# The S5 transfer tables laid out contiguously by a ScalarE copy, and the low halves of all head weights subtracted on VectorE, in a one-core hybrid decoder step

## The chip, the core and the metric

The program runs on one core of one Trainium2 chip. The metric is the time of one execution on the device in microseconds, as the median of several executions. Each engine (TensorE as PE, with its weight loads shown apart as PEld; VectorE as DVE; ScalarE as ACT; GpSimd as POOL; SyncE as SP, which only issues DMAs here) works through its own instructions in the order in which the program lists them, and waits where an input or a buffer isn't ready.

## What is computed

One decoder layer for 512 prompt tokens (with 16 meta tokens ahead of them) and 8 running sequences of 4 tokens, at width 1024. Two branches run beside each other on the projected input and are merged: HGRN2, a gated linear recurrence with 8 heads, and S5, a diagonal state-space model in 64 groups of 16 channels and 64 states. After them comes PEER, a mixer that picks 16 of 16384 single-neuron experts per head and token. Cut to the part around the change:

```python
proj = rmsnorm(x, norm1_w) @ w_in
q, f, i, g, u, ga, gb = split(proj)
o, s_new = hgrn2_scan(silu(q), 1 - fg, i, log(fg), s_hg)      # 8 heads of 128
y, x_re, x_im = s5_scan(u, ...)   # x_t = a_bar * x_(t-1) + b_bar u_t ;  y = Re(c x) + d u
x = x + (sigmoid(ga) * br_a + sigmoid(gb) * br_b) @ w_out
x = x + peer(rmsnorm(x, norm2_w), ...)
```

S5 is computed in blocks of 8 time steps. For each group a 128x128 table T (8 steps x 16 channels squared) gives what the inputs of a block add to the outputs of the same block, a table W gives what the state at the block's start adds, and AT gives the block's addition to the state.

## The kernel before

**Weight stream.** All dense products use 128x1024 weight tiles in fp32, split into two fp32r halves: `wh` is the tile cast on ACT (L434) and `wl` is tile minus `wh` (L435), on the engine that the job names. `Stream.run` takes the jobs in order. Job i multiplies its 8 blocks (`products`, L469: wh by hi, wh by lo, wl by hi, with two column halves each). Before its first product it issues the fetch, the cast and the subtraction for job i+1. `wh`, `wl` and the raw tile have two buffers each. After each quarter of a job the stream ticks two lists of background generators, `bg` and `fill`, and each tick issues one piece of such a generator to all engines.

**Jobs.** First come 8 jobs of S5's input u, then the 8 heads with 4 jobs each (F, Q, V, G: gate, query, value, output gate; F1 is the F job of head 1), then 8 each of GA, BA, GB, GLU, BB and WO. `N_EV = 1` puts the subtraction of head 0 on VectorE; heads 1 to 7 have it on GpSimd.

**Beside the heads.** While a head's jobs run, `bg` works on the head before (`head`): seven levels of `aps` matmuls on PE (L605, L612), each followed on DVE by the update of `h_qF` (L624) and `f_kB` (L625) that the next level's matmul reads. `fill` runs `s5_setup`, which makes the tables for eight sets of 8 groups: E, AT and W on DVE (L369, L371), a 128x128 piece `T7`, and then eight DMAs (`load(Ts[o % 2]...)`) that place shifted pieces of T7 in T with the group innermost, so that neighbouring elements of one group's table are 4 elements (16 bytes) apart. T goes to DRAM as it is (`Td`). `fill` also runs `rotations`, many small GpSimd operations (L286 to L293).

**S5 units.** From GA3 on, 16 units of four groups each run in `bg` (`s5_units`). A unit loads T, W, AT and its inputs, and its output is

```python
for g in range(4):
    mm(pyv[:, g], T[:, g], U[:, g, m0 : m0 + ny], start=True, stop=False)
    mm(pyv[:, g], W[:, g], xs[:, g, m0 : m0 + ny], start=False, stop=True)
```

with T or W as the stationary operand (L790, L791). In fp32 each of these matmuls runs as two passes. T is read through a view with a step of 4 elements; W is contiguous.

Of the kernel before, what the change touches and what calls it, by code (L numbers as in the profile page):

```python
# [8 lines left out]
F32 = mybir.dt.float32  # L9
# [10 lines left out]
P = 128  # L20
# [6 lines left out]
G = 64  # L27
# [63 lines left out]
def body(tc, a):  # L91
    nc = tc.nc
    mm = nc.tensor.matmul
    V, PO, AC = nc.vector, nc.gpsimd, nc.scalar
# [8 lines left out]
    def load(dst, src):  # L103
        nc.sync.dma_start(dst, src)
# [90 lines left out]
    Td = dram.tile([8, P, 2, 4 * P], F32, name="Td")  # L195
# [8 lines left out]
    def s5_setup(pm, qr):  # L204
# [42 lines left out]
            V.tensor_scalar(c, c, -2.0, 1.0, ALU.mult, ALU.add)  # L247
        t1 = sm("t1")
        q = pool(s5, "s5c", 1, True)
        Ts = [q.tile([P, 2, 8, 16, 4], F32, name=f"T{i}") for i in range(2)]  # L250
        u1, u2 = (T.rearrange("p a s c g -> p (a s c g)")[:, : 4 * G].rearrange("p (n g) -> p n g", g=G) for T in Ts)

        def cmul(outr, outi, ar, ai, br, bi, n):
            a, b = u1[:, :n], u2[:, :n]
# [77 lines left out]
        for e in (1, 2, 4):  # L332
            o, i = slice(8 - 2 * e, 8 - e), slice(8 - e, 8)
# [4 lines left out]
        V.tensor_copy(s5c["a4s"][64:128], pim[64:128, 4])  # L338
        V.tensor_scalar(s5c["a4s"][0:64], pim[0:64, 4], -1.0, None, ALU.mult)

        for T in Ts:
            PO.memset(T, 0.0)

        def params(o):
            r = {}
# [3 lines left out]
            return r  # L349

        def store(o):
            load(Td[o], Ts[o % 2].rearrange("p a s c g -> p a (s c g)"))

        nx = params(0)
        yield
# [1 line left out]
        for o in range(8):  # L357
            gs = slice(8 * o, 8 * o + 8)
            p, nx = nx, (params(o + 1) if o < 7 else None)
            V.tensor_scalar(p["b2"], p["b2"], sgn, None, ALU.mult)  # L360
            V.tensor_scalar(p["ct1"], p["ct1"], nsgn, None, ALU.mult)
            V.tensor_scalar(p["ct2"], p["ct2"], -1.0, None, ALU.mult)
            AT = q.tile([P, 8, P], F32, name="AT", tag="AT", bufs=2)
            E = q.tile([P, 8, 8, 16], F32, name="E", tag="E")
            W = q.tile([P, 8, 8, 16], F32, name="W", tag="W", bufs=2)
            for x, u, w, cr, ci in ((E, "b1", "b2", gr[:, :, gs], gi[:, :, gs]), (W, "ct1", "ct2", pr[:, 1:, gs], pim[:, 1:, gs])):
                xv, tmp = x.rearrange("p g s c -> p s g c"), AT.rearrange("p g (s c) -> p s g c", s=8)
                for dst, pp, cc in ((xv, p[u], cr), (tmp, p[w], ci)):
                    V.tensor_tensor(dst, pp.unsqueeze(1).to_broadcast([P, 8, 8, 16]), cc.unsqueeze(3).to_broadcast([P, 8, 8, 16]), ALU.mult)  # L369
                    yield  # L370
                V.tensor_tensor(xv, xv, tmp, ALU.add)  # L371
                yield
            Ec = E.rearrange("p g s c -> p g (s c)")
            T7 = q.tile([P, 2, 16, 4], F32, name="T7", tag="T7")
            T7v = T7.rearrange("p a c g -> p a g c")
            if o > 0:
                store(o - 1)
            V.tensor_tensor(T7v, p["dsk"].rearrange("p (a g) c -> p a g c", a=2), ident[:, 112:128].unsqueeze(1).unsqueeze(1).to_broadcast([P, 2, 4, 16]), ALU.mult)
            yield
            pt = pm.tile([P, 8, 16], F32, name="pt", tag="m")  # L380
            for i in range(8):
                mm(pt[:, i], Ec[:, i], p["ct1"][:, i], start=True, stop=True)
            V.tensor_tensor(T7v, T7v, pt.rearrange("p (a g) c -> p a g c", a=2), ALU.add)
            for hf in range(2):
                pt = pm.tile([P, 4, P], F32, name="pt", tag="m")
                for i in range(4):
                    nc.tensor.transpose(pt[:, i], Ec[:, 4 * hf + i], ident)
                AC.copy(AT[:, 4 * hf : 4 * hf + 4], pt)
                yield
            load(Wd[o], W.rearrange("p g s c -> p g (s c)"))  # L390
            for s in range(8):
                load(Ts[o % 2][0 : 16 * (s + 1), :, s], T7[16 * (7 - s) : 128])
                if s % 2:
                    yield
            load(ATd[o], AT)
# [304 lines left out]
    def s5_units(ph, pm, sp, Ud, Yd, units):  # L700
# [25 lines left out]
        for n_, u in enumerate(units):  # L726
            o, hf = u // 2, u % 2
            g4 = slice(4 * hf, 4 * hf + 4)
            gs = slice(4 * u, 4 * u + 4)
            r, nxt = nxt, None  # L730
            U, rc, rs = r["U"], r["rc"], r["rs"]
            T, W, xs = st("T", P), st("W", P), st("xs", nxs)
            load(T.rearrange("p g n -> p (g n)"), Td[o][:, hf])
            T = T.rearrange("p g n -> p (g n)").rearrange("p (n g) -> p g n", g=4)
            load(W, Wd[o][:, g4])
            if ph.sample:
                xw0 = st("xw0", 8)
                load(xs[:, :, nch:nxs], a["x0"][:, gs])
                load(xw0, a["x0w"][:, gs])
            if n_ + 1 < len(units):  # L740
                nxt = loads(units[n_ + 1])
            px = pm.tile([P, 512], F32, name="px", tag="m")
            pxv = px[:, : 4 * nu].rearrange("p (g n) -> p g n", n=nu)
            for g in range(4):
                mm(pxv[:, g], r["AT"][:, g], U[:, g], start=True, stop=True)
            X = st("X", nu)
            AC.copy(X, pxv)
            d0 = st("d0", nch)
            PO.tensor_copy(d0, s5c["rho"][:, gs].unsqueeze(2).to_broadcast([P, 4, nch]))
            PO.memset(d0[:, :, 0:1], 0.0)  # L750
            if ph.first:
                PO.memset(xs[:, :, 0:1], 0.0)
            else:
                PO.tensor_copy(xs[:, :, 0], sstate[:, gs])
            yield

            def swap(src):
                t = pm.tile([P, 512], F32, name="pxs", tag="m")
                tv = t[:, : 4 * nch].rearrange("p (g n) -> p g n", n=nch)
                mm(tv, T_["perm"], src, start=True, stop=True)  # L760
                return tv

            xw = swap(X[:, :, :nch])
            Z, t2, z, zc = st("Z", nch), st("t2", nch), st("z", nch), st("zc", nch)
            V.tensor_tensor(Z, X[:, :, :nch], rc[:, :, 1 : nch + 1], ALU.mult)
            V.tensor_tensor(t2, xw, rs[:, :, 1 : nch + 1], ALU.mult)
            V.tensor_tensor(Z, Z, t2, ALU.subtract)
            if not ph.first:
                z0 = st("z0", 1)
                V.tensor_tensor(z0[:, :, 0], sstate[:, gs], s5c["rho"][:, gs], ALU.mult)  # L770
                V.tensor_tensor(Z[:, :, 0], Z[:, :, 0], z0[:, :, 0], ALU.add)
            V.tensor_tensor_scan(z.rearrange(fl), d0.rearrange(fl), Z.rearrange(fl), 0.0, ALU.mult, ALU.add)
            V.tensor_tensor(zc, z, rc[:, :, 1 : nch + 1], ALU.mult)
            if ph.sample:
                f, f2 = st("xf", 8), st("xf2", 8)
                PO.tensor_tensor(f, xs[:, :, nch:nxs], s5c["a4r"][:, gs].unsqueeze(2).to_broadcast([P, 4, 8]), ALU.mult)
                PO.tensor_tensor(f2, xw0, s5c["a4s"][:, gs].unsqueeze(2).to_broadcast([P, 4, 8]), ALU.mult)
                PO.tensor_tensor(f, f, f2, ALU.add)
                PO.tensor_tensor(f, f, X[:, :, nch + 8 : nch + 16], ALU.add)
                PO.dma_start(a["o_ssm_s"][:, gs], f)  # L780
            yield
            zw = swap(z)
            V.tensor_tensor(t2, zw, rs[:, :, 1 : nch + 1], ALU.mult)
            V.tensor_tensor(xs[:, :, 1:nch], zc[:, :, : nch - 1], t2[:, :, : nch - 1], ALU.add)
            V.tensor_tensor(sstate[:, gs], zc[:, :, nch - 1], t2[:, :, nch - 1], ALU.add)
            yield
            py = pm.tile([P, 512], F32, name="py", tag="m")
            pyv = py[:, : 4 * ny].rearrange("p (g n) -> p g n", n=ny)
# [3 lines that stand above are left out]
            y = st("y", ny)  # L792
            AC.activation(y, pyv, AF.Gelu)
            AC.dma_start(Yd[o].rearrange("s c f -> (s c) f")[:, 4 * hf * ny : 4 * (hf + 1) * ny], y.rearrange(fl))
            yield
# [4 lines left out]
    S5_WAIT = 4  # L800
    Y_WAIT = 3
    N_RATE = 1
    N_EV = 1
    PIECES, B_RATE = 4, 0.85


    def network(ph, keep_h2, wq, es, sq):
# [80 lines left out]
        for h in range(H):  # L888
            if h and ujobs:
                jobs.append(ujobs.pop(0))  # L890
            E = V if h < N_EV else PO
            jobs += [(F0 + h, hpair, N, head_done(h, "f"), E), (Q0 + h, hpair, NO, head_done(h, "q"), E),
                     (V0 + h, hpair, N, head_done(h, "v"), E), (G0 + h, hpair, NO, head_done(h, "sg"), E)]
        n_heads = len(jobs)
# [884 lines left out]
```

## Time and profile before

| | |
|---|---|
| median of 3 runs | 2215.28 us (2215.02 to 2215.9) |
| the profiled execution | 2217.47 us, of which 2215.7 us from the first to the last instruction |
| PE busy | 2104.8 us, 95% of the span |
| DVE / ACT / POOL busy | 71% / 38% / 37% |
| mean granted TensorE clock | 0.98 of full speed |

Busy time of PE says that a matmul was in the array's pipeline, not that it ran at its best rate. [...]

### The profile page before, as it was taken

To read this page: it belongs to the slowest core of one execution; us is meant where nothing else is said; L and a number is where in the kernel's file an instruction comes from. 1 tells how busy PE (TensorE), PEld (TensorE's weight loads), DVE (VectorE), ACT (ScalarE), POOL (GpSimd) and SP (SyncE) were. 2 spreads that over 40 slices of the span, in tenths; PEclk is the share of its full clock that TensorE was granted. 3 is DMA by queue.
4 is the path that set the end of the run, shared out by engine and by line. 5 is a ranking of instruction groups with operands and counts; after the bars stand their busy time and mean duration, and the time that the engine had idled before them with its cause. 6 is when DMAs were issued, how large, how long until landed. Compare 5 with 4: busy or idle time off the path is not lost. (4 is left out here: it accounts for less than half of the span.)

```text
span 2215.7 us, 34563 instructions
## 1 busy us (share of the span) xinstructions
PE 2104.8 (95%) x13085; PEld 1938.3 (87%) x13085; DVE 1579.0 (71%) x3056; ACT 848.8 (38%) x1583; POOL 818.5 (37%) x904
## 2 busy tenths in 40 slices
PE   7899998999999998999899999999999999999995
PEld 6889898899999998999899887989888888888884
DVE  6867677655335423799999688868877888788777
ACT  3323232333113323333477544344433434433443
POOL 3487762223443334575066211212222222222221
PEclk9999999998999999999999999999999999999998
DMA  5433334325654243222356899989988999889984
GB/s 152 119 108 121 118 121 152 117 97 177 188 155 125 86 146 125 97 89 74 110 213 257 313 340 307 333 291 351 345 317 317 335 340 337 323 316 336 334 297 164
DMA packets 199814, 478.90 MB, mean 216 GB/s; under 512 B 53440, under 2 KB 114752, under 8 KB 176096
## 3 DMA queue, kind: packets, MB, share of 16 engines
q1 hardware_dynamic: 169136, 278.50, 37.6%
q0 software_dynamic: 24752, 170.67, 20.5%
q10 hardware_dynamic: 5760, 27.53, 3.1%
q8 instruction: 103, 1.69, 0.3%
q14 instruction: 63, 0.52, 0.1%
HBM read 419.42 MB, written 54.46 MB: 214 GB/s over the span
## 5 line engine op out<-in xcount | busy, mean ns | idle before, releaser
L469 PE MATMUL gps<-pr,wh 128*128 128x272 f32 (+1 forms) x3328 | 587.1, 299 | 5.6 <-DVE pr L483 3.1
L469 PEld LDWEIGHTS gps<-pr,wh 128*128 128x128 f32 x3328 | 484.2, 193 | 14.2 <-issue 4.2
L1482 DVE TENSOR_TENSOR tlo<-traw,thi 128x1024 fp32r<-128x1024 f32 x241 | 299.0, 1241 | 119.4 <-ACT thi L1474 118.9
L1338 POOL DMA_INDIRECT uv<-in_uv,ei x128 | 186.1, 1454 | 534.9 <-DVE acc L1359 527.3
L469 PE MATMUL gps<-pr,wl 128*128 128x272 f32 (+1 forms) x1664 | 355.7, 294 | 7.3 <-POOL wl L435 6.2
L1500 PE MATMUL hps<-pr,tlo 128*128 128x384 f32 x1024 | 347.4, 339 | 14.5 <-DVE tlo L1482 13.6
L1498 PE MATMUL hps<-pr,thi 128*128 128x384 f32 x1024 | 350.1, 342 | 1.5 <-ACT thi L1474 1.2
L435 POOL TENSOR_TENSOR wl<-wraw,wh 128x1024 fp32r<-128x1024 f32 x88 | 217.8, 2475 | 348.5 <-ACT wh L434 342.6
L1499 PE MATMUL hps<-pr,thi 128*128 128x384 f32 x1024 | 343.8, 336 | 0.0
L469 PEld LDWEIGHTS gps<-pr,wl 128*128 128x128 f32 x1664 | 268.9, 193 | 8.4 <-POOL wl L435 6.7
L1474 ACT CAST thi<-traw 128x1024 fp32r<-128x1024 f32 x256 | 266.0, 1040 | 26.4 <-PE eacc L1558 18.1
L1558 PE MATMUL eacc<-thi,ghi 128*128 128x512 f32 x768 | 241.5, 395 | 7.7 <-ACT ghi L482 6.6
L1558 PE MATMUL eacc<-tlo,ghi 128*128 128x512 f32 x768 | 241.3, 395 | 3.4
L1558 PE MATMUL eacc<-thi,glo 128*128 128x512 f32 x768 | 237.4, 390 | 0.0
L1359 DVE SCALAR_TENSOR_TENSOR acc<-uv,w,acc 128x1024 f32<-128x1024 f32 x158 | 202.4, 1281 | 33.9 <-ACT w L1354 33.9
L1353 ACT ACTIVATE w<-w 128x1 f32<-128x1 f32 x160 | 32.5, 203 | 478.7 <-DVE uv L1352 478.7
L1500 PEld LDWEIGHTS hps<-pr,tlo 128*128 128x128 f32 x1024 | 192.5, 188 | 20.8 <-DVE tlo L1482 19.6
L1498 PEld LDWEIGHTS hps<-pr,thi 128*128 128x128 f32 x1024 | 192.6, 188 | 10.2 <-ACT thi L1474 4.4
L1499 PEld LDWEIGHTS hps<-pr,thi 128*128 128x128 f32 x1024 | 192.7, 188 | 3.5
L1352 DVE SCALAR_TENSOR_TENSOR uv<-uv,h 128x1024 f32<-128x1024 f32 x160 | 195.0, 1219 | 0.3 <-DMA uv<-in_uv,ei_None 0.3
L1558 PEld LDWEIGHTS eacc<-tlo,ghi 128*128 128x128 f32 x768 | 141.5, 188 | 46.3 <-DVE tlo L1482 17.8
L1558 PEld LDWEIGHTS eacc<-thi,ghi 128*128 128x128 f32 x768 | 140.9, 188 | 41.7 <-ACT ghi L482 17.7
(409 smaller groups left out, 3013.6 us busy)
## 6 DMA issues: line engine op xcount, KB each, us to landing
traw<-in_uT SPq DMA_DIRECT2D x128, 512.0 KB
traw<-in_uv SPq DMA_DIRECT2D x128, 512.0 KB
wraw<-in_W SPq DMA_DIRECT2D x104, 512.0 KB
Wt<-wb ACTq DMA_DIRECT2D x24, 1024.0 KB
wt<-Wt SPq DMA_DIRECT2D x15, 1536.0 KB
st<-in_state_hgrn SPq DMA_DIRECT2D x8, 512.0 KB
Wd<-W SPq DMA_DIRECT2D x8, 512.0 KB
ATd<-AT SPq DMA_DIRECT2D x8, 512.0 KB
```

What stands on the lines that cost most here:

```text
L435: E.tensor_tensor(wl, r3, wh, ALU.subtract)
L469: mm(ps[:, b, :w], x[:, k], y[:, k, b * w : b * w + w], start=(k == 0 and x is wh and y is hi), stop=(k == KT - 1 and x is wl))
L1338: PO.indirect_dma_start(out=uvs[j], out_offset=None, in_=a["uv"], in_offset=bass.IndirectOffsetOnAxis(ap=ei[:, k : k + 1], axis=0))
L1352: V.scalar_tensor_tensor(out=uv[:, 0:D], in0=uv[:, 0:D], scalar=1.0, in1=h2, op0=ALU.mult, op1=ALU.mult, accum_out=w)
L1353: AC.activation(w, w, AF.Gelu)
L1359: V.scalar_tensor_tensor(acc, uv[:, D:], w, acc, ALU.mult, ALU.add)
L1474: AC.copy(x, t)
L1482: (PO if kind == "u" and e < sum(AQ) else V).tensor_tensor(y, raws.pop((kind, e)), x, ALU.subtract)
L1498: mm(ps[:, :nt], x[:, ks], hi[:, k, cs], start=(k == 0), stop=False)
L1499: mm(ps[:, :nt], x[:, ks], lo[:, k, cs], start=False, stop=False)
L1500: mm(ps[:, :nt], y[:, ks], hi[:, k, cs], start=False, stop=(k == KT - 1))
L1558: mm(accs[d][:, b], l[:, ds_], r[:, b * 512 : b * 512 + 512], start=st, stop=en)
```

## The change

1. `s5_setup` keeps one T rather than two. When a set's table is complete, ACT copies it to a new tile `Tc` in which each group's 128 columns are contiguous, and `Tc` is what goes to DRAM. `s5_units` then reads T without the strided view. The next set's DMAs into T wait for the copy.
2. `N_EV` is gone: the subtraction for the 28 jobs of heads 1 to 7 is on VectorE. Nothing else in the stream is altered.

```diff
-        Ts = [q.tile([P, 2, 8, 16, 4], F32, name=f"T{i}") for i in range(2)]
...
+        T = q.tile([P, 2, 8, 16, 4], F32, name="T")
+        Tc = q.tile([P, 2, 4, P], F32, name="Tc")
...
-        for T in Ts:
-            PO.memset(T, 0.0)
+        PO.memset(T, 0.0)
...
         def store(o):
-            load(Td[o], Ts[o % 2].rearrange("p a s c g -> p a (s c g)"))
+            AC.copy(Tc, T.rearrange("p a s c g -> p a g (s c)"))
+            load(Td[o], Tc.rearrange("p a g n -> p a (g n)"))
...
             for s in range(8):
-                load(Ts[o % 2][0 : 16 * (s + 1), :, s], T7[16 * (7 - s) : 128])
+                load(T[0 : 16 * (s + 1), :, s], T7[16 * (7 - s) : 128])
...
             load(T.rearrange("p g n -> p (g n)"), Td[o][:, hf])
-            T = T.rearrange("p g n -> p (g n)").rearrange("p (n g) -> p g n", g=4)
...
-            E = V if h < N_EV else PO
+            E = V
```

PE's order is the same in both programs, and SP's too but for the source of the eight stores. The other three engines differ by what is added and removed: ACT gains 8 copies, DVE gains 28 subtractions, POOL loses 28 subtractions and one memset. Lines from 250 on stand two lines lower in the new kernel up to L733, so L371 there is L369 here, L626 is L624, L437 is L435.

On VectorE, at job G0, where the set-up of S5's first tables stands among the head's work (`f_sg` is G0's output), the order before is

```order
L369 TENSOR_TENSOR E<-d_b_1219,gr 128x8x8x16
L369 TENSOR_TENSOR AT<-d_b_1221,gi 128x8x8x16
L371 TENSOR_TENSOR E<-E,AT 128x8x8x16
L369 TENSOR_TENSOR W<-d_ct_1223,pr 128x8x8x16
L879 SCALAR_TENSOR_TENSOR f_sg<-f_th,gps 128x544
L369 TENSOR_TENSOR AT<-d_ct_1225,pim 128x8x8x16
```

and after the change

```order
L371 TENSOR_TENSOR E<-d_b_1218,gr 128x8x8x16
L437 TENSOR_TENSOR wl<-wraw,wh 128x1024
L371 TENSOR_TENSOR AT<-d_b_1220,gi 128x8x8x16
L373 TENSOR_TENSOR E<-E,AT 128x8x8x16
L371 TENSOR_TENSOR W<-d_ct_1222,pr 128x8x8x16
L879 SCALAR_TENSOR_TENSOR f_sg<-f_th,gps 128x544
L437 TENSOR_TENSOR wl<-wraw,wh 128x1024
```

The first `wl` there is that of F1, the second that of Q1; each stands between two pieces of S5's tables.

On VectorE, at the start of job Q4, the subtraction for V4 comes in ahead of the third level of head 3's chain. Before:

```order
L369 TENSOR_TENSOR W<-d_ct_2430,pr 128x8x8x16
L624 TENSOR_TENSOR h_qF<-h_qF,h_g_3183 128x64x4
L625 TENSOR_TENSOR f_kB<-f_kB,h_g_3183 128x66x4
L630 COPY_PREDICATED h_att<-k_masks,aps 128x64x4
L639 TENSOR_TENSOR h_g_3229<-h_g_3183 128x66
```

and after:

```order
L371 TENSOR_TENSOR W<-d_ct_2430,pr 128x8x8x16
L437 TENSOR_TENSOR wl<-wraw,wh 128x1024
L626 TENSOR_TENSOR h_qF<-h_qF,h_g_3184 128x64x4
L627 TENSOR_TENSOR f_kB<-f_kB,h_g_3184 128x66x4
L632 COPY_PREDICATED h_att<-k_masks,aps 128x64x4
L641 TENSOR_TENSOR h_g_3230<-h_g_3184 128x66
```

The `wl` needs ACT's cast of the same tile, so what stands behind it in the chain now waits for that cast as well.

On ScalarE, the copy of the last set comes between the cast for V7 and the copy that the levels of head 6 need (L629, L627 before). After the change:

```order
L436 CAST wh<-wraw 128x1024
L353 COPY Tc<-T 128x1024
L629 COPY h_sq<-f_kB 128x256
L877 ACTIVATE f_th<-gps 128x544
L436 CAST wh<-wraw 128x1024
```

The copy needs the eight DMAs of T's last set; the rows behind it are the same as before.

## Rows read from the trace of the kernel before

**Rows 1.** The page: the span, and PE's busy time, share of the span and instructions.
```profile
span 2215.7 us, 34563 instructions
PE 2104.8 (95%) x13085; PEld 1938.3 (87%) x13085; DVE 1579.0 (71%) x3056; ACT 848.8 (38%) x1583; POOL 818.5 (37%) x904
```

**Rows 2.** The busy time by stage (stretch, its length, then for PE, PEld, DVE, ACT and POOL the busy us and the instructions, then the granted TensorE clock, the DMA share and GB/s): the heads, the S5 units, and all from the end of the router's queries on.
```profile
80.00:455.00 375.00, 348.13 (x2613) 329.03 (x2612) 253.18 (x489) 117.34 (x256) 225.76 (x434) 0.95 0.38 121
...
495.00:665.00 170.00, 166.17 (x1110) 159.18 (x1109) 75.71 (x162) 37.59 (x63) 73.56 (x142) 0.95 0.57 174
...
1040.00:2215.70 1175.70, 1121.79 (x5849) 991.84 (x5849) 954.47 (x1322) 518.63 (x1002) 317.11 (x220) 0.99 0.81 297
```

**Rows 3.** Groups of instructions by line in 495 to 665 us: the matmuls with T stationary, their weight loads, and the weight loads of W (count, then busy us, mean ns of one, and the idle time before them).
```profile
L790 PE MATMUL py<-s_U,s_T 128*128 128x72 f32 x128 | 39.3, 391 | 0.0
L790 PEld LDWEIGHTS py<-s_U,s_T 128*128 128x128 f32 x128 | 34.9, 321 | 0.4 <-issue 0.2
L791 PEld LDWEIGHTS py<-s_xs,s_W 128*128 128x128 f32 x128 | 21.8, 212 | 0.5 <-DVE s_xs L784 0.5
```

**Rows 4.** PE in order of time, in one S5 unit at the full clock: start us, us, then the two passes of one group with T (L790) and with W (L791).
```profile
561.01 0.63 PE L790 MATMUL py<-s_U,s_T 128*128 128x72 f32 x2
561.47 0.39 PE L791 MATMUL py<-s_xs,s_W 128*128 128x72 f32 x2
561.69 0.63 PE L790 MATMUL py<-s_U,s_T 128*128 128x72 f32 x2
```

**Rows 5.** The same in a unit at the half clock.
```profile
517.06 0.66 PE L790 MATMUL py<-s_U,s_T 128*128 128x72 f32 x2
517.51 0.63 PE L791 MATMUL py<-s_xs,s_W 128*128 128x72 f32 x2
517.93 0.66 PE L790 MATMUL py<-s_U,s_T 128*128 128x72 f32 x2
```

**Rows 6.** Busy time of two stretches among the S5 units (columns as in group 2; the granted clock is the third number from the end).
```profile
510.00:530.00 20.00, 19.63 (x100) 18.74 (x100) 6.91 (x17) 5.80 (x10) 5.49 (x13) 0.66 0.38 119
530.00:545.00 15.00, 14.99 (x88) 13.72 (x87) 8.07 (x20) 3.03 (x5) 7.35 (x17) 0.89 0.63 194
```

**Rows 7.** PE's waits in the heads' stage, 80 to 455 us: who waited for whom, us in total, times, longest.
```profile
PE aps L605 <- DVE f_kB L625: 11.8, 6, 5.1
PE gps L469 <- POOL wl L435: 5.5, 1, 5.5
PE gps L469 <- DVE f_q L879: 2.3, 1, 2.3
PE aps L605 <- DVE h_qF L594: 2.1, 3, 1.0
```

**Rows 8.** Groups of instructions in 80 to 455 us: the subtraction on VectorE (head 0) and on GpSimd (heads 1 to 7, and two of GA), with busy us and mean ns of one.
```profile
L435 DVE TENSOR_TENSOR wl<-wraw,wh 128x1024 fp32r<-128x1024 f32 x3 | 3.8, 1254 | 0.0
...
L435 POOL TENSOR_TENSOR wl<-wraw,wh 128x1024 fp32r<-128x1024 f32 x30 | 78.8, 2625 | 129.1 <-ACT wh L434 129.1
```

**Rows 9.** The same view with shapes kept apart: the update of `h_qF` in the chain's levels of 256 columns.
```profile
L624 DVE TENSOR_TENSOR h_qF<-h_qF,h_g 128x256 f32<-128x256 f32 x35 | 23.5, 673 | 25.7 <-PE aps L605 14.5 <-PE aps L612 10.8
```

**Rows 10.** DVE and POOL in order of time around F1's subtraction.
```profile
104.86 1.26 DVE L369 TENSOR_TENSOR E<-d_b,gr 128x1024 f32<-128x1024 f32 x1
...
109.97 2.34 POOL L435 TENSOR_TENSOR wl<-wraw,wh 128x1024 fp32r<-128x1024 f32 x1
110.21 3.17 DVE L369 TENSOR_TENSOR AT<-d_ct,pim 128x1024 f32<-128x1024 f32 x1
```

**Rows 11.** DVE, POOL and PE in order of time around G6's subtraction (`vm` is a GpSimd product for head 5's samples).
```profile
370.43 3.34 POOL L435 TENSOR_TENSOR wl<-wraw,wh 128x1024 fp32r<-128x1024 f32 x1 [6.70 <-ACT wh L434]
371.49 2.56 DVE L624 TENSOR_TENSOR h_qF<-h_qF,h_g 128x256 f32<-128x256 f32 x1
373.73 2.07 POOL L650 TENSOR_TENSOR vm<-h_v,c_vmask 96x1024 fp32r<-96x1024 f32 x1
373.97 2.12 DVE L625 TENSOR_TENSOR f_kB<-f_kB,h_g 128x264 f32<-128x264 f32 x1
...
376.24 0.66 PE L605 MATMUL aps<-h_qF,f_kB 128*128 128x64 f32 x2 [5.11 <-DVE f_kB L625]
```

**Rows 12.** Busy time of two stretches of 5 us that follow PE's two longest waits (columns as in group 2).
```profile
110.00:115.00 5.00, 2.64 (x11) 2.64 (x12) 4.68 (x3) 0.00 (x0) 4.84 (x6) 0.50 0.29 102
...
375.00:380.00 5.00, 3.76 (x17) 3.79 (x18) 4.97 (x8) 0.00 (x0) 0.80 (x1) 0.53 0.67 215
```

**Rows 13.** DVE and ACT in order of time around V4's subtraction.
```profile
268.84 0.41 DVE L624 TENSOR_TENSOR h_qF<-h_qF,h_g 128x256 f32<-128x256 f32 x1
...
269.36 1.03 ACT L434 CAST wh<-wraw 128x1024 fp32r<-128x1024 f32 x1
...
271.23 3.29 DVE L371 TENSOR_TENSOR W<-W,AT 128x1024 f32<-128x1024 f32 x1
```

**Rows 14.** ACT and SP in order of time at the last set of tables.
```profile
420.19 1.03 ACT L434 CAST wh<-wraw 128x1024 fp32r<-128x1024 f32 x1
...
426.76 0.61 SPq L104 DMA_DIRECT2D ATd<-AT  x1
428.34 0.41 ACT L627 COPY h_sq<-f_kB 128x256 f32<-128x256 f32 x1 [7.12 <-DVE f_kB L625]
...
429.88 0.33 SPq L104 DMA_DIRECT2D Td<-T  x1
```

More of the change, by code (lines that the diff above doesn't have):

```diff
@@ L249, in s5_setup @@
         q = pool(s5, "s5c", 1, True)
-        Ts = [q.tile([P, 2, 8, 16, 4], F32, name=f"T{i}") for i in range(2)]
-        u1, u2 = (T.rearrange("p a s c g -> p (a s c g)")[:, : 4 * G].rearrange("p (n g) -> p n g", g=G) for T in Ts)
+        T = q.tile([P, 2, 8, 16, 4], F32, name="T")
+        Tc = q.tile([P, 2, 4, P], F32, name="Tc")
+        Tf = T.rearrange("p a s c g -> p (a s c g)")
+        u1, u2 = (Tf[:, 4 * G * i : 4 * G * (i + 1)].rearrange("p (n g) -> p n g", g=G) for i in range(2))
         def cmul(outr, outi, ar, ai, br, bi, n):
@@ L802, in body @@
     N_RATE = 1
-    N_EV = 1
     PIECES, B_RATE = 4, 0.85
```

## The prediction

> **What bounds the kernel now.** I read the page first: PE is busy for 2104.8 of 2215.7 us, so 111 us are left in which it stands, and no other engine is near its limit [rows 1]. A change pays here only if it shortens PE's own work, takes away one of its waits, or keeps its clock up. Then the busy time by stage, to see which of the three there is where the edits are. In the heads (80 to 455 us) PE is busy for 348 of 375 us, so it stands for 27 us, with the granted clock at 0.95; DVE is busy for 253 us and so stands for 122 us. In the S5 units (495 to 665 us) PE stands for 4 us only, clock 0.95. From 1040 us to the end PE is busy for 1122 of 1176 us [rows 2]. PE's waits say who ends the 27 us in the heads: DVE's `f_kB` and `h_qF`, 13.9 us in 9 waits, and once GpSimd's `wl`, 5.5 us [rows 7]. Then the groups and the order in time, for prices.
>
> **T's layout: the matmuls.** PE does 64 groups (16 units of 4) with T and with W, two passes each. A weight load of T takes 321 ns and one of W 212 ns [rows 3]: same size, same type, the step of 4 elements is the difference. What PE pays is read from starts: at the full clock the two T passes hold it for 561.47 - 561.01 = 0.46 us, the two W passes for 561.69 - 561.47 = 0.22 us [rows 4]. With T contiguous I give it W's price: 0.24 us less per group. At the half clock T holds PE for 0.45 us and W for 0.42 us [rows 5], so there the layout costs next to nothing. A tenth of this stage runs at the half clock (17 of 170 us, below), so I leave out 7 of the 64 groups. 57 x 0.24 = 13.7 us; I take 13. The bounds are 0 and 64 x 0.24 = 15 us. PE hardly waits in this stage, so what its instructions lose in length the stage loses too.
>
> [...]
>
> **T's layout: the clock.** Between 510 and 530 us the granted clock is 0.66, between 530 and 545 us 0.89 [rows 6]: a share of 0.68 and 0.22 at the half clock, 13.6 and 3.3 us, which cost about half of themselves, 8.4 us together. A burst of T and W matmuls stands ahead of both and inside the first. Denser bursts may leave the clock up. Bounds 0 and 8.4 us; nothing in the trace decides, and I take half, 4 us.
>
> **T's layout: the copies.** Eight ACT copies of 128x1024. The nearest row is ACT's cast of that size, 1.03 us [rows 14]; with a step of 16 bytes it may double as T's loads did, so 8 to 16 us on an engine that is busy for 117 of 375 us in the heads [rows 2]. Seven stand where T's DMAs landed long ago, and cost PE nothing, unless they push a cast for the stream: its cover is a whole job of PE. The last doesn't. It follows the cast that ends at 421.2 us and needs the last DMA into T, issued just before the ATd store at 426.8 us; the Td store, which waits for the same landing, went at 429.9 us [rows 14]. With the raw tile free some 1.2 us sooner (below) the copy starts at about 428.7 and ends at 429.8. Queued behind it on ACT are `h_sq` (428.3 us before), the tanh of Q7 and the cast for G7; PE's next level of head 6 waits for the first, DVE's `f_q` and the new `wl` for the others. I price that at 2 us (0 to 4). Where SP's store of Td now waits for a copy, its next DMA follows a good deal later in the trace, so I cost that at nothing; if a tile's fetch were held up there, it would have most of a job, some 10 us, before PE needs it. One memset less on POOL costs and brings nothing.
>
> **The subtractions: what DVE gains and loses.** Added: 28 x 1.25 us = 35 us; taken from POOL: 28 x 2.63 us = 74 us [rows 8]. The two don't simply add, since a POOL subtraction holds up DVE. A table product that takes 1.26 us takes 3.17 us when it starts 0.24 us after a `wl` on POOL and ends just after it [rows 10]; `h_qF`, 0.41 us alone [rows 13], takes 2.56 us beside G6's `wl` [rows 11], and over 35 levels it averages 0.67 us [rows 9]: 35 x 0.26 = 9 us for this one shape. Two such hits of about 2 us stand in groups 10 and 11; at one per `wl` the relief is at most 28 x 2 = 56 us, and at least those 9 us. So DVE's load changes by something between 26 us more and 21 us less, with 122 us of idle time to take it. I take it as even and look at places.
>
> F1: its `wl` on POOL ran from 109.97 to 112.31 us, queued behind rotations, and PE waited 5.5 us for it [rows 7, 10]. On DVE it stands right behind the E product that ends at 106.12 us [rows 10], so it is there at 107.4 us: 5 us back.
>
> G6: PE waited 5.1 us for `f_kB`. `h_qF` lost 2.1 us to G6's `wl`, then `f_kB` 1.7 us to `vm`, which was queued behind that `wl` [rows 11]. Without it on POOL `vm` runs when its inputs are there, long before; the new `wl` stands behind Q6's `f_q`, after this stretch. 3.8 us back.
>
> The other `f_kB` and `h_qF` waits, 13.9 - 5.1 = 8.8 us in 8 places [rows 7], lie mostly at a V or Q job beside a POOL `wl`. An own 1.25 us replaces a hit of about 2 us there: I take 4 us back (0 to 8.8).
>
> Against these: DVE now waits for ACT's cast ahead of each `wl`, and the head's chain stands behind it. At V4 `h_qF` began at 268.84 us, while the cast ended only at 270.39 us [rows 13]; the chain's step starts at 270.4 + 1.25 = 271.6, 2.8 us late, and gets 2.1 us back at the table product that took 3.29 us [rows 13]. With DVE's idle time as cover most of this doesn't reach PE; I charge 3 us (0 to 10) over the 28.
>
> **The clock in the heads.** 0.95 over 375 us means 37 us at the half clock, 19 us lost [rows 2]. After the two longest waits it stood at 0.50 and 0.53 [rows 12]: about 5 us of loss follow from these two. I take 4 us back (0 to 9).
>
> **The sum.** 13 + 4 - 2 + 5 + 3.8 + 4 - 3 + 4 = 28.8 us. The work behind starts when the work before ends, and PE is the bound to the end, so I carry it through: 2217.5 - 28.8 = 2188.7 us for an execution like the profiled one. That one lies 2.2 us above the median of the runs, so I predict a median of **2187 us**. No measurement of this kernel can tell less than 0.2% (4.4 us) from no change.
>
> **The rivals.**
> - *The heads give nothing.* The 35 us on DVE and the waits for casts eat what the hits and the two long waits give back, and the clock stays. For it: DVE is the engine that PE waits for. Then 13 us from T and some 2 us of clock: 2200 us. Chance 0.2.
> - *T's loads don't get faster.* [...] The heads alone then, 28.8 - 13 - 4 = 12 us: 2203 us. Chance 0.06.
> - *More comes back.* The half-clock stretches beside S5 go (8.4 us), those after waits too (9 us), the chain is never late: 13 + 8 + 5 + 4 + 6 + 9 - 2 = 43 us, 2172 us. Chance 0.12.
> - *DVE becomes the bound of the heads: slower.* Each of the 28 subtractions lands whole on the path, 35 us, and the hits come from rotations and `vm` as before. Less 13 us for T: 22 us more, 2237 us. It decides once the chain's delays exceed the 122 us of DVE's idle time where they fall, that is if PE's waits for `f_kB` rise from 12 to over 25 us. Chance 0.04.
> - *Nothing to measure*: this loss at half its size cancels T's gain. 2215 us, chance 0.03.
>
> **How the numbers follow.** The forecast keeps 0.55, 2180 to 2195 us by its own bounds. From 2174 us (most of the third rival left out) to 2204 us (the first two rivals inside) is the range; about 2 in 10 lies outside. All cases but the last two are faster by over 0.2%: faster 0.93, same 0.03, slower 0.04.
>
> **What the changed kernel's profile would show.** L790's weight loads at 205 to 215 ns, not 321, and a T pair at 0.22 to 0.25 us on PE at the full clock; the S5 stage shorter by 13 to 20 us. 28 subtractions of 1.2 to 1.3 us more on DVE, `h_qF` of 256 columns near 0.45 us, DVE's busy time in the heads within 25 us of before. No PE wait for a head's `wl` over 1 us, `f_kB` waits under 6 us in total, the heads' stage shorter by 8 to 18 us. One ACT wait of some 7 us at the last `Tc`. The prediction is wrong if T's loads stay slow, or if PE's waits for `f_kB` grow.

## The result, and the profile after the change

| | before | after |
|---|---|---|
| median of 5 runs | 2215.02 us | 2198.56 us |
| the profiled execution | 2217.47 us | 2195.1 us |
| span, mean granted clock | 2215.7 us, 0.980 | 2193.2 us, 0.985 |

The ratio is 0.9927 (95% interval 0.9912 to 0.9942): 16.5 us less in the medians, 22.4 us less between the two profiled executions. The forecast was a median of 2187 us, so the kernel came out 11.6 us slower than forecast: inside the range of 2174 to 2204 us, but outside the 2180 to 2195 us that the forecast gave itself. Of the change's 14 executions on record four took 2205 to 2208 us and ten 2194 to 2200 us, so a median of five or six depends on how many of the four it holds.

The page after the change, its span and busy times (against [rows 1]):

```profile
span 2193.2 us, 34559 instructions
...
PE 2083.8 (95%) x13085; PEld 1916.0 (87%) x13085; DVE 1570.8 (72%) x3084; ACT 864.5 (39%) x1591; POOL 754.6 (34%) x875
```

PE is still the bound. Its busy time fell by 21.0 us and the span by 22.5 us, so nearly all of the gain is PE's own work getting shorter; the time in which it stands fell only from 110.9 to 109.4 us. DVE's busy time is 8 us lower in spite of 28 more subtractions, and POOL's is 64 us lower.

Busy time by stage (columns as in [rows 2]):

```profile
80.00:455.00 375.00, 349.63 (x2635) 328.26 (x2635) 247.33 (x520) 132.67 (x264) 161.75 (x405) 0.97 0.38 122
495.00:665.00 170.00, 165.04 (x1273) 158.44 (x1272) 78.82 (x170) 43.58 (x71) 80.94 (x147) 1.00 0.64 192
```

In the heads PE stands for 25.4 us of the same 375 us, against 26.9 before. In the S5 units the granted clock is 1.00, against 0.95. So the heads gave almost nothing, and the S5 units gave the gain. The program's own marks say the same: the time at which ACT begins to read a job's result, from the order in time of each trace (half-clock: length of the half-clock stretches between 455 and 660 us). Half clock is a granted clock of 0.50: in steps of 1 us from 80 to 660 us the trace of before reads 1.00 in 516 and 0.50 in 42, and the other 22, between the two, each lie beside a step at 0.50. The 13.6 us at the half clock that the prediction takes from a mean of 0.66 over 20 us [rows 6] rest on this reading.

| kernel | F1 | Q4 | G7 (last head) | first GB | G7 to GB | half-clock |
|---|---|---|---|---|---|---|
| before | 121.9 | 278.3 | 449.8 | 658.6 | 208.8 | 20.5 |
| after | 116.3 | 275.9 | 446.9 | 636.8 | 189.9 | 3.4 |

From the first GB job to the end it is 1557.1 us before and 1556.4 us after. The 22.5 us are therefore 2.9 us in the heads, 18.9 us from the last head to the first GB job, and 0.7 us behind them.

The groups of the S5 units after the change, 495 to 665 us (against [rows 3]):

```profile
L791 PE MATMUL py<-s_U,s_T 128*128 128x72 f32 x128 | 24.2, 270 | 0.0
L791 PEld LDWEIGHTS py<-s_U,s_T 128*128 128x128 f32 x128 | 19.7, 191 | 0.4
L792 PEld LDWEIGHTS py<-s_xs,s_W 128*128 128x128 f32 x128 | 19.4, 192 | 0.8 <-DVE s_xs L785 0.8
```

T's weight load went from 321 to 191 ns and now is W's. PE in order of time in one unit at the full clock (against [rows 4]):

```profile
544.90 0.39 PE L791 MATMUL py<-s_U,s_T 128*128 128x72 f32 x2
545.13 0.39 PE L792 MATMUL py<-s_xs,s_W 128*128 128x72 f32 x2
545.35 0.39 PE L791 MATMUL py<-s_U,s_T 128*128 128x72 f32 x2
```

From start to start T's two passes hold PE for 545.13 - 544.90 = 0.23 us, against 0.46 us in [rows 4]. Summed over all 128 passes, from each start to the next matmul's start, T held PE for 29.0 us before and 14.5 us after.

PE's waits in the heads, 80 to 455 us (against [rows 7]):

```profile
PE aps L614 <- ACT h_sq L629: 10.0, 7, 2.9
PE aps L607 <- DVE f_kB L627: 5.7, 7, 1.3
PE aps L607 <- DVE h_qF L596: 3.5, 2, 1.7
PE gps L471 <- DVE f_q L879: 2.3, 1, 2.3
PE gps L471 <- DVE wl L437: 2.2, 3, 1.1
```

The 5.5 us wait for GpSimd's `wl` is gone and `f_kB` fell from 11.8 to 5.7 us. A new wait has taken their place: 10.0 us for `h_sq`, the copy on ACT that turns `f_kB` into the operand of the chain's later levels. Before, it stood at 1.8 us:

```profile
PE aps L612 <- ACT h_sq L627: 1.8, 3, 0.8
```

### The profile page after: what moved, and what is told of

Same layout as the page of the kernel before. It is cut to its first block, busy times and chain, and to the rows that moved or that the text cites. A ratio compares the mean times of both kernels' runs of the same rounds, so it can differ in the third digit from the quotient of the medians.

```text
span 2193.2 us, 34559 instructions
## 1 busy us (share of the span) xinstructions
PE 2083.8 (95%) x13085; PEld 1916.0 (87%) x13085; DVE 1570.8 (72%) x3084; ACT 864.5 (39%) x1591; POOL 754.6 (34%) x875
## 5 line engine op out<-in xcount | busy, mean ns | idle before, releaser
L1500 PE MATMUL hps<-pr,tlo 128*128 128x384 f32 x1024 | 347.7, 340 | 14.5 <-DVE tlo L1482 13.6
L437 POOL TENSOR_TENSOR wl<-wraw,wh 128x1024 fp32r<-128x1024 f32 x60 | 144.1, 2401 | 247.0 <-ACT wh L436 240.0
L1498 PEld LDWEIGHTS hps<-pr,thi 128*128 128x128 f32 x1024 | 192.7, 188 | 10.2 <-ACT thi L1474 4.5
L1558 PEld LDWEIGHTS eacc<-thi,ghi 128*128 128x128 f32 x768 | 140.9, 188 | 40.5 <-ACT ghi L484 16.5
```

Of the source, the lines that this page charges most:

```text
L437: E.tensor_tensor(wl, r3, wh, ALU.subtract)
L1498: mm(ps[:, :nt], x[:, ks], hi[:, k, cs], start=(k == 0), stop=False)
L1500: mm(ps[:, :nt], y[:, ks], hi[:, k, cs], start=False, stop=(k == KT - 1))
L1558: mm(accs[d][:, b], l[:, ds_], r[:, b * 512 : b * 512 + 512], start=st, stop=en)
```

## The experiments

Two theories went into the first four. A: the layout carries the change, and moving the subtractions brings 2 to 4 us. B: each half brings some 10 us, and the copies on ACT eat the heads' half.

**The layout alone.** The whole change with the subtractions of heads 1 to 7 back on GpSimd:

```diff
-            E = V
+            E = V if h < 1 else PO
```

> The contiguous T with its copies alone; the subtractions of heads 1 to 7 are back on GpSimd. Theory A (the layout carries the change): the heads end as late as before or up to 2 us later (last copy on ScalarE), then the S5 stage is 18 to 21 us shorter, 13 from the T matmuls and the rest from a granted clock of 0.99 to 1.00 in it instead of 0.95; about 2196 to 2200 us, as fast as the whole change. Theory B (each half brings some 10 us): S5 stage 12 to 13 us shorter with the clock still near 0.95, about 2203 us.

Measured: a median of 2207.84 us (2202.03 to 2212.36), ratio 0.9963 (0.9949 to 0.9977), 7.6 us less than before and slower than either theory says. The heads were worse than either theory has them, in a profiled execution of 2211.91 us, 4 us above the median. G7 was read at 456.6 us, 6.8 us later than before; from there to the first GB job it took 197.6 us, 11.2 us less. T's passes held PE for 14.9 us, so the layout's own 14 us were all there, and more was lost around them. Two stretches of this run's S5 units, 500 to 520 and 520 to 535 us (columns as in [rows 2]):

```profile
500.00:520.00 20.00, 15.90 (x95) 13.91 (x95) 15.67 (x21) 6.90 (x10) 10.06 (x18) 0.91 0.80 234
520.00:535.00 15.00, 15.00 (x84) 14.28 (x84) 4.78 (x13) 5.29 (x8) 0.81 (x1) 0.67 0.06 21
```

PE stood for 4.1 of 20 us at the first units, and then the granted clock fell to 0.67. So the contiguous T doesn't by itself keep the clock up: this kernel has it too, and had 13.7 us at the half clock in this stage. In the heads the copies on ACT and GpSimd's subtractions add up: 5.1 us for `f_kB` at G6's place as in [rows 11], and 2.8 us for `h_sq` behind the last copy. The granted clock there was 0.94, against 0.95 before.

**The subtractions alone.** The kernel before with all of them on VectorE:

```diff
-            E = V if h < N_EV else PO
+            E = V
```

> The subtractions of heads 1 to 7 on VectorE alone; T as in the kernel before (strided, two buffers, no copies). Theory A: F1's wait of 5.5 us goes, most of it is given back later in the heads by waits of TensorE for h_sq and f_kB; the heads end 2 to 4 us earlier, the S5 stage is as before (T weight loads 321 ns), 2211 to 2214 us. Theory B (the copies on ScalarE ate the heads' gain): without copies the heads end 8 to 12 us earlier, about 2205 us.

Measured: 2210.3 us (2203.51 to 2217.73), ratio 0.9973 (0.9955 to 0.9991), 5.1 us less than before. G7 was read at 443.6 us, 6.2 us earlier than before, between the two theories; S5's stage took 209.3 us, as before. PE's waits in the heads of this run:

```profile
PE aps L612 <- ACT h_sq L627: 7.3, 5, 2.9
PE aps L605 <- DVE f_kB L625: 5.2, 6, 1.2
PE aps L605 <- DVE h_qF L594: 3.4, 2, 1.7
```

The wait for `h_sq` is here without a single copy of T. So most of it comes with the subtraction's place on VectorE. The two halves alone give 7.6 and 5.1 us, 12.7 together, and the whole change 16.5 (14.3 when it ran again, below): about additive in the medians. In the marks of one profile each they don't add up as well: in the heads 6.8 us lost and 6.2 gained against 2.9 gained, from G7 to GB 11.2 gained and 0.5 lost against 18.9 gained.

**No copies.** The whole change, T stored as it was from two buffers and read as if it were contiguous, so that S5 adds numbers of a wrongly ordered table:

```diff
-            AC.copy(Tc, T.rearrange("p a s c g -> p a g (s c)"))
-            load(Td[o], Tc.rearrange("p a g n -> p a (g n)"))
+            load(Td[o], Ts[o % 2].rearrange("p a s c g -> p a (s c g)"))
```

> The whole change, but the eight copies on ScalarE are left out: T is stored with the group innermost from two buffers as before, and read as if it were contiguous, so the numbers that S5 adds are those of a wrongly ordered table; no time depends on them. Theory A: the copies cost 1 to 2 us in all (the last one), 2196 to 2198 us. Theory B: the copies cost 6 us or more, 2192 us or less, and the wait of TensorE for the level of the chain behind the last copy is gone.

Measured: 2192.32 us (2188.78 to 2194.33), ratio 0.9892 (0.987 to 0.9913), some 6 us below the whole change's median. G7 was read at 443.5 us, first GB at 634.9. That is theory B's size. All five executions, 2188.8 to 2194.3 us, lie below all 14 of the change. But the profiled one, 2194.33 us, took hardly less than the profiled ones of the change, so no profile shows where the 6 us went; what it shows is that PE's waits for `h_sq` are 6.8 us, against 10.0. The five profiles of the whole change (below) have G7 at 443.7 to 449.1 us, mean 446.6, so the 3.1 us at G7 between one profile and that mean are no more than their spread. Two places show the copies at work, though, and one of them the prediction didn't have; the other is the last copy, which it had. ACT, DVE and PE in order of time at job Q4, after the change:

```profile
273.63 0.41 ACT L629 COPY h_sq<-f_kB 128x256 f32<-128x256 f32 x1 [8.46 <-DVE f_kB L627]
273.94 2.03 ACT L353 COPY Tc<-T 128x1024 f32<-128x1024 f32 x1
275.87 0.62 ACT L877 ACTIVATE f_th<-gps 128x544 f32<-128x544 f32 x1
...
276.53 0.72 DVE L879 SCALAR_TENSOR_TENSOR f_q<-f_th,gps 128x544 f32<-128x544 f32 x1 [1.97 <-ACT f_th L877]
277.47 1.23 DVE L437 TENSOR_TENSOR wl<-wraw,wh 128x1024 fp32r<-128x1024 f32 x1 [0.22 <-ACT wh L436]
...
279.93 0.71 PE L614 MATMUL aps<-h_qF,h_sq 128*128 128x128 f32 x4 [1.41 <-ACT h_sq L629]
```

The copy had its data long before. It takes 2.03 us and holds up the tanh of Q4's result by about that; `f_q` on DVE waits 1.97 us for the tanh, `wl` waits for the cast behind it, the head's chain stands behind `wl`, and PE waits 1.41 us for the next level. In the run without copies, and in the one with the subtractions alone, the tanh follows `h_sq` at once and this wait of PE is absent.

**The subtraction behind the background's work.** The whole change, but from head 1 on the subtraction for job i+1 is issued after the first quarter of job i and the background pieces that follow it, not ahead of job i's first product. The cast keeps its place; the fetch of the next tile into the same raw buffer, which follows the subtraction, moves with it.

```diff
             AC.copy(wh, r3)
-            E.tensor_tensor(wl, r3, wh, ALU.subtract)
...
                         bg.tick(self.rate)
                         fill.tick(self.frate)
+                        self.split_low()
```

> The whole change, but the subtraction of the next job stands on VectorE behind the first quarter's pieces of the background work, not ahead of them (heads 1 to 7); the cast on ScalarE stays where it is. If what eats the heads' gain is that the chain's step stands on VectorE behind a subtraction that still waits for its cast: TensorE's waits for h_sq fall from 10 us to under 4 us, the heads end 5 to 8 us earlier than in the whole change, about 2191 us. If the chain is late for other reasons (its own inputs, table pieces ahead of it): within 2 us of the whole change, about 2198 us.

Measured: 2190.87 us (2186.02 to 2203.17), ratio 0.9891 (0.9863 to 0.9919). G7 was read at 438.7 us, 8 us earlier than the mean of the whole change and 5 us earlier than its earliest profile. PE's wait for `h_sq` is 3.5 us in 7. Job Q2 shows how. After the change, DVE, ACT and PE in order of time:

```profile
181.31 0.72 DVE L879 SCALAR_TENSOR_TENSOR f_q<-f_th,gps 128x544 f32<-128x544 f32 x1 [1.04 <-ACT f_th L877]
182.25 1.36 DVE L437 TENSOR_TENSOR wl<-wraw,wh 128x1024 fp32r<-128x1024 f32 x1 [0.22 <-ACT wh L436]
183.53 0.67 DVE L626 TENSOR_TENSOR h_qF<-h_qF,h_g 128x256 f32<-128x256 f32 x1
...
185.31 0.71 PE L614 MATMUL aps<-h_qF,h_sq 128*128 128x128 f32 x4 [2.33 <-ACT h_sq L629]
```

The same place with the subtraction behind the chain's step:

```profile
181.96 0.72 DVE L896 SCALAR_TENSOR_TENSOR f_q<-f_th,gps 128x544 f32<-128x544 f32 x1 [1.04 <-ACT f_th L894]
182.60 0.49 DVE L643 TENSOR_TENSOR h_qF<-h_qF,h_g 128x256 f32<-128x256 f32 x1
...
183.89 1.21 DVE L453 TENSOR_TENSOR wl<-wraw,wh 128x1024 fp32r<-128x1024 f32 x1
...
184.20 0.71 PE L631 MATMUL aps<-h_qF,h_sq 128*128 128x128 f32 x4 [0.60 <-ACT h_sq L646]
```

With `wl` ahead, its 0.22 us of waiting and its own 1.36 us stand before the level, and PE waits 2.33 us; with `wl` behind it PE waits 0.60 us. How much of the gain in the heads is the wait for the cast and how much the subtraction's own time, no run separates.

The place of G6's old stall, in job Q6, is another matter. After the change, DVE, ACT and PE in order of time:

```profile
367.87 0.42 DVE L627 TENSOR_TENSOR f_kB<-f_kB,h_g 128x264 f32<-128x264 f32 x1
...
368.44 1.08 PE L607 MATMUL aps<-h_qF,f_kB 128*128 128x64 f32 x8 [0.96 <-DVE f_kB L627]
368.65 1.22 DVE L371 TENSOR_TENSOR AT<-d_ct,pim 128x1024 f32<-128x1024 f32 x1
...
369.90 1.22 DVE L373 TENSOR_TENSOR W<-W,AT 128x1024 f32<-128x1024 f32 x1
...
371.05 0.71 DVE L879 SCALAR_TENSOR_TENSOR f_q<-f_th,gps 128x544 f32<-128x544 f32 x1
371.68 1.22 DVE L437 TENSOR_TENSOR wl<-wraw,wh 128x1024 fp32r<-128x1024 f32 x1
372.81 0.42 DVE L626 TENSOR_TENSOR h_qF<-h_qF,h_g 128x256 f32<-128x256 f32 x1
...
373.60 0.40 ACT L629 COPY h_sq<-f_kB 128x256 f32<-128x256 f32 x1 [6.90 <-DVE f_kB L627]
374.05 0.71 PE L614 MATMUL aps<-h_qF,h_sq 128*128 128x128 f32 x4 [2.92 <-ACT h_sq L629]
```

The old stall of 5.11 us on `f_kB` [rows 11] is 0.96 us after the change. But the next level stands behind two table products, `f_q` and `wl`, and PE waits 2.92 us there. In the run with `wl` behind the level these two waits are 1.95 and 0.21 us; its eight `aps` matmuls behind the first wait took 1.78 us, so PE came to the second later. The run with F1's subtraction ahead again, below, has the same order at this place, and there these eight took 1.08 us.

What the run with the subtraction behind the background's work lost was F1's: its subtraction stood behind a piece of S5's tables, and PE waited 3.0 us for it.

**The change again, the kernel before again.** No edit; the question is whether the clock in the S5 units belongs to the program.

> The changed kernel once more, to see whether its S5 stage is at the full clock in every execution. If the contiguous T keeps the clock up: at most one short half-clock stretch between the end of the heads and the first GB job, and that stage 18 to 20 us shorter than before. If the clock there depends on the execution: 7 to 17 us at the half clock as in the kernel with the layout alone (13.6 us), and the stage only 11 to 15 us shorter. The median is about 2198 us in either case.

> The kernel before once more, for the same question: 20.5 us at the half clock between 461 and 660 us in the first profile. If that belongs to the program (strided T): 14 us or more again. If it belongs to the execution: it may be as low as 3 to 7 us, and the stage only little shorter, since T's matmuls take 0.45 us at either clock. Median 2215 us.

Measured: the change 2201.92 us (2196.66 to 2207.27), ratio 0.9938 (0.9916 to 0.996); before 2215.14 us (2212.34 to 2218.62), ratio 0.9998. The second profile of the change has 3.4 us at the half clock between 455 and 660 us and 189.9 us from G7 to GB, as the first. The second profile of before has 10.2 us at the half clock instead of 20.5, and 207.9 us from G7 to GB instead of 208.8. So ten us fewer at the half clock gave 0.9 us there. From starts, T's passes hold PE for 26.9 us in both profiles between these marks, as a pair takes 0.46 us at the full clock and 0.45 us at the half clock [rows 4, 5]; the stream's products, W and AT hold it for 3.2 us less, and PE's waits are 2.1 us longer. The length at the half clock isn't fixed by the program either.

**F1's subtraction ahead again.** As the run with the subtraction behind the background's work, from Q1 on only:

```diff
-        s.lates = range(N_U0 + 4, n_heads)
+        s.lates = range(N_U0 + 5, n_heads)
```

> As the run with the subtraction behind the first quarter's background work, but F1's subtraction ahead of it as in the whole change, since F1's stood behind a piece of S5's tables that waits for a DMA and TensorE waited 3.0 us for it. If the gain of that run is the chain's and F1's loss is separate: F1 3 us earlier, heads end 13 to 14 us earlier than before the change, about 2188 us. If F1's 3 us only shift where the chain waits: as that run, 2191 us.

Measured: 2195.2 us (2186.79 to 2201.52), ratio 0.9908 (0.9882 to 0.9933). F1 was read at 116.0 us, 3.7 us earlier than in the run it changes, but at G7 (437.2 us) only 1.5 us of that were left: most of F1's gain is taken up later. The profiled execution, 2187.38 us, is near the first forecast, but the median is above both. PE's busy time in the heads, and its waits there:

```profile
80.00:455.00 375.00, 355.60 (x2702) 335.16 (x2702) 254.26 (x537) 134.72 (x267) 169.90 (x407) 0.97 0.39 123
```

```profile
PE aps L624 <- DVE f_kB L644: 6.2, 6, 2.0
PE aps L631 <- ACT h_sq L646: 3.9, 6, 1.8
PE aps L624 <- DVE h_qF L613: 3.6, 3, 1.7
```

PE stands for 19.4 of 375 us here, against 25.4 us with the whole change and 26.9 before. At the place of G6's old stall, with `wl` behind the level:

```profile
362.88 1.08 PE L624 MATMUL aps<-h_qF,f_kB 128*128 128x64 f32 x8 [1.95 <-DVE f_kB L644]
...
367.36 0.71 PE L631 MATMUL aps<-h_qF,h_sq 128*128 128x128 f32 x4 [1.80 <-ACT h_sq L646]
```

That is 3.75 us in two waits, against 3.88 us after the change: the order brought next to nothing there. The gain stands at other places: the wait of 2.33 us at Q2 is 0.39 us, none at Q4 is over 0.7 us where the change has 0.93, 1.25 and 1.41 us, and at Q7 0.93 us stand for 1.19 and 1.63.

**The contiguous layout by DMA.** As the run above, with two T tiles in the contiguous order and no copy on ACT:

```diff
-        T = q.tile([P, 2, 8, 16, 4], F32, name="T")
-        Tc = q.tile([P, 2, 4, P], F32, name="Tc")
+        Ts = [q.tile([P, 2, 4, 8, 16], F32, name=f"T{i}") for i in range(2)]
...
-                load(T[0 : 16 * (s + 1), :, s], T7[16 * (7 - s) : 128])
+                load(Ts[o % 2][0 : 16 * (s + 1), :, :, s], T7[16 * (7 - s) : 128])
```

> As the run before in this list, and the eight copies on ScalarE are gone: the DMAs place T7's pieces in the contiguous layout themselves, 64 bytes in one piece instead of 256, from two T tiles. If the copies cost 3 us in the heads and the small pieces are covered: heads end 3 us earlier still, about 2185 us. If the small pieces load the queues so that weight tiles come late: TensorE waits for casts and subtractions in the heads, 2195 us or more.

Measured: 2191.75 us (2186.38 to 2204.05), ratio 0.9899 (0.9873 to 0.9926). G7 was read at 439.4 us, first GB at 630.8 us. The small pieces raise the DMA share in the heads from 0.39 to 0.43, and PE's waits for `wl` there are 1.9 us, against 2.3 us in the run above. Taking the copies away brings nothing more once the chain doesn't stand behind `wl`: G7 is 2.2 us later than with them. These three kernels, 2190.9 to 2195.2 us, have lower medians than both before and the change; this one and the change ran beside each other, 2191.75 and 2201.92 us, with intervals of the ratio that overlap a little. Among the three the order isn't settled.

**Three more profiles of the change.** No edit.

> The changed kernel again: its times fall into 2195 to 2199 us (mean granted clock 0.985) and 2205 to 2208 us (0.980 to 0.982), and both profiles so far are of the first kind. One of these three looks should catch the second kind. If the S5 stage decides: 10 to 14 us at the half clock between the heads' end and the first GB job, as in the kernel with the layout alone, and that stage 5 to 8 us longer; the heads as before. If not: the same stage at full clock, and the half clock in the heads or in what follows.

> Second of three looks at the changed kernel with the same question: does an execution of 2205 us or more lose its 10 us in the S5 stage, at the half clock, or elsewhere?

> Third of three looks at the changed kernel with the same question: does an execution of 2205 us or more lose its 10 us in the S5 stage, at the half clock, or elsewhere?

Measured: 2197.78, 2194.79 and 2196.73 us. All three have 0 to 3.4 us at the half clock in the S5 units and 188.8 to 190.5 us from G7 to GB (G7 at 449.1, 445.0 and 448.2 us). None of the three took 2205 us or more, so where such an execution loses its 10 us stays open.

## Why the prediction held, and where its steps missed

It held by its range: 2198.56 us lies beside the 2200 us of its first rival, to which it gave 0.2, and not in the 2180 to 2195 us to which it gave 0.55. T and its clock came as said or better, `f_kB`'s waits fell under the 6 us that it named, but the heads' stage is 2.9 us shorter where it named 8 to 18.

**T's matmuls: right, 13 us said, 14.5 measured.** The rows of W were the right price. I left out 7 groups for the half clock of the old S5 units, and the new program didn't have that stretch. The 321 ns and the 191 ns are for the same 128 columns of fp32 (319 ns from 545 to 655 us before, 192 ns from 545 to 630 us after, both at a clock of 1.00), so a step of 16 bytes was not free here.

**The clock in S5: 4 us said, some 4 to 5 measured, for a reason only half mine.** From G7 to GB the profiled stage is 18.9 us shorter. The sum over starts inside that stretch (the last unit ends behind it) gives 13.6 us for T, which leaves 5.3 us: the stream's own products took 3.5 us less, W 1.5 us and AT's products 1.0 us, all the rest some half a microsecond more. Against the second profile of before the stage is 18.0 us shorter. None of these has an edit; I read most of it as what more of the full clock is worth. Two runs bear on that: at 10.2 us of half clock each, the stage takes 207.9 us with the strided T (before, second profile) and 193.6 us with the contiguous one (the subtraction behind the background's work), so 14.3 us come at the same length of half clock; and the five profiles of the change, with 0 to 3.4 us of it, take 188.8 to 190.5 us. "Cost about half of themselves, 8.4 us" was too high, because the old T passes lost nothing at the half clock (0.45 us a pair, against 0.46 us [rows 4, 5]). And the layout alone did not keep the clock up (13.7 us at the half clock). With the contiguous T it stayed at 1.00 in the first units after the change, where PE's longest wait is 0.7 us (490 to 530 us), and fell to 0.67 in the run with the layout alone, where the longest is 1.8 us; but in the first profile of before it fell for 13.7 us with no PE wait there over 0.4 us, so what keeps it up isn't shown.

**The copies: 2 us said, 2.6 us by PE's waits and some 6 us by the medians measured.** "Seven stand where T's DMAs landed long ago, and cost PE nothing, unless they push a cast" failed at the exception: at Q4 the copy pushed a tanh, and `f_q`, the cast, `wl` and the chain with it. Each copy took 2.05 us, the upper end of my bounds. T's loads, though, had not doubled as I wrote: they are 321 ns against 212 ns [rows 3], and what is twice W's is T's hold on PE [rows 4]. The last one waited 5.93 us for T's DMA, where I had said some 7, and PE waited 1.19 us for the `h_sq` behind it. (The 1.63 us for the next level are there without copies too, 1.59 us.) With the 1.41 us at Q4 that makes 2.6 us; where the rest of the 6 us goes is open.

**F1: right, 5 us said, 5.6 measured** (121.9 to 116.3 us; the five profiles of the change have 115.5 to 118.3, the second of before 123.8). Its `wl` ended at 107.86 us, where 107.4 us was said. Not all of it hangs on the engine, though: in the run with the layout alone F1 was read 2.4 us earlier with its subtraction still on POOL. Before, four of POOL's rotations ahead of that subtraction took 1.1 to 1.2 us each beside the table products on DVE, where the others of their size took 0.2 us; in that run only one did, and POOL came to them 0.35 us sooner (104.48 against 104.83 us) and DVE to its products 0.56 us later (105.42 against 104.86 us). Whether the missing memset did that wasn't tried.

**G6: the stall went, the gain didn't come.** This step failed: 3.8 us said, 1.2 measured. I wrote that "the new `wl` stands behind Q6's `f_q`, after this stretch", and followed the stretch no further. The 4.2 us that `f_kB` gave back were followed by 2.92 us for `h_sq` one level later. Between the two levels DVE has two table products (2.4 us), `f_q` (0.7 us) and now `wl` (1.2 us). Before, the table products and `f_q` stood there too, but PE came late to that level, out of its stall of 5.11 us [rows 11] and at a clock of 0.53 [rows 12], and didn't wait; and with `wl` behind the level 1.80 us of the wait are still there. The half clock came as before, 6.8 us of it from 375 us on.

**The other waits and the cast: 4 back and 3 lost were said; the loss was the larger.** This is the step that cost the heads most: the 3 us for "the head's chain stands behind it", with DVE's idle time as cover. PE's waits for `f_kB` and `h_qF` gave back 4.7 us (13.9 to 9.2) where my terms for G6 and the others say 7.8; its waits for `h_sq`, which aren't in [rows 7], grew by 8.2 us (1.8 to 10.0). In the run with the subtraction behind the chain's step they are 3.5 us. With the subtractions alone G7 came 6.2 us earlier, of which F1 had 5.1 us. All the rest of the heads, G6 and the clock with it, gave 1.1 us, where my terms say 3.8 + 4 - 3 + 4 = 8.8. The groups of 80 to 455 us after the change, shapes kept apart (busy us, mean ns of one, idle time of the engine before them):

```profile
L437 DVE TENSOR_TENSOR wl<-wraw,wh 128x1024 fp32r<-128x1024 f32 x31 | 39.8, 1284 | 14.5 <-ACT wh L436 14.5
...
L353 ACT COPY Tc<-T 128x1024 f32<-128x1024 f32 x8 | 16.4, 2050 | 6.1 <-DMA T<-T 5.9 <-issue 0.2
L626 DVE TENSOR_TENSOR h_qF<-h_qF,h_g 128x256 f32<-128x256 f32 x35 | 16.1, 461 | 24.7 <-PE aps L614 13.3 <-PE aps L607 11.4
```

The same group of subtractions from Q1 on, in the run with F1's ahead again:

```profile
L453 DVE TENSOR_TENSOR wl<-wraw,wh 128x1024 fp32r<-128x1024 f32 x27 | 33.0, 1222 | 4.0 <-ACT wh L435 4.0
```

DVE's load did come out as even as said: 253 us before, 247 after, `h_qF` at 461 ns and not 673 [rows 9]. But load was not the question. DVE stood 14.5 us for casts ahead of its subtractions, and what stands behind them in its order stood with it; with the subtraction behind the chain's step this idle time is 4.0 us.

**The sum.** The profiled gain is 22.4 us where 28.8 were said: some 9 us too many for the heads, 2 too few for S5, 1 for what follows. The other 5 us of the miss are the step from a profiled execution to the median: I took off 1.7 us, while this kernel's profiled execution lies 3.5 us below its median. Of the rivals, the first (the heads give nothing, 2200 us) is nearest to what happened, though S5 gave its clock too.

## What to carry to other kernels

Put an operation that only feeds the next job behind the operations that PE waits for in this one: VectorE took its instructions in the program's order here, and the 14.5 us that it stood for casts ahead of its subtractions held up what came behind them (4.0 us with the subtraction behind the chain's step). A stall that is removed must be followed to the next instruction that PE needs; here seven tenths of it came back one level later, in a wait for another engine. Lay out a stationary operand contiguously, and price it by a matmul of the same shape that already is: W's pair took 0.22 us [rows 4], and T's takes 0.23 us after the change.

## What the runs showed of the hardware

- A step of 16 bytes between the fp32 columns of the stationary operand made its load 321 ns long instead of 191 ns [rows 3], and a pass held PE for 0.23 us instead of 0.11 us at the full clock [rows 4]. At the half clock it took the same 0.23 us, while a pass of W went from 0.11 to 0.21 us [rows 4, 5].
- A 128x1024 fp32 copy on ScalarE that read with the same step took 2.05 us; the cast of a contiguous tile of that size took 1.03 us [rows 14].
